# A two-layer HGRN2 and sliding-window-attention trunk: the framework's order of work taken from its time-line picture

## The chip, the cores and the metric

The kernel runs on one core of a Trainium2 chip. A core has four engines that compute: TensorE (PE, matrix products; its loads of stationary operands are shown apart as PEld), VectorE (DVE), ScalarE (ACT) and GpSimd (POOL). SyncE (SP) starts DMA transfers. Each engine works through a list of its own, in order, and instructions of different engines wait for each other by semaphores. The metric is the time of one execution on the device, in microseconds (us), as the median of the runs; beside it, one execution was recorded by the hardware profiler. All quoted rows come from that profile.

## The reference

x has 512 rows of 1024 numbers, fp32. Two layers (DEPTH = 2) each compute

```python
h = rms_norm(x, g_pre)
proj = jnp.einsum('bsd,de->bse', h, w_in)
q_h, f_h, i_h, z_h, q_a, k_a, v_a, z_a = jnp.split(proj, SPLIT_POINTS, axis=-1)
o_h = hgrn2(q_h, f_h, i_h, lb)
o_h = rms_norm(o_h, g_head).reshape(B, S, HG_WIDTH).astype(z_h.dtype) * jax.nn.silu(z_h)
...
o_a = sliding_window_attention(q_a, k_a, v_a, sinks).astype(z_a.dtype) * jax.nn.silu(z_a)
y = jnp.einsum('bse,ed->bsd', jnp.concatenate([o_h, o_a], axis=-1), w_out)
return x + rms_norm(y, g_post)
```

`w_in` has 6400 columns: 1024 each for the recurrence's queries, forget logits, inputs and gate, 1024 for the attention's queries, 128 each for its keys and values, 1024 for its gate. `w_out` maps 2048 to 1024. The recurrence has 8 heads with a 128 x 128 state, S_t = diag(f_t) S_(t-1) + (1 - f_t) i_t^T and o_t = S_t^T q_t. The attention has 16 query heads and 2 key heads of width 64, a causal window of 128, rotary positions and one sink logit per head.

## The kernel before, in words

**Projections.** All weights come as fp32 pieces of 128 x 512 (`raw`, four buffers). Each piece is split in two parts whose sum is the number: ScalarE rounds it to the matmul's type (`whi`, line 189), VectorE forms the rest (`wlo`, line 190). A ring of nine `whi` and nine `wlo` tiles holds the pieces. The activations are split alike (`hhi`, `hlo`, `ops`). Each product is three matmuls of 128 x 128 by 128 x 512 into a PSUM bank `pj` (line 302, three banks): high by high, high by low, low by high. A `Unit` is one output tile of such a projection; `step` writes the next three matmuls, and two units may run interleaved.

**Order in the program.** `ORDER` gives the order of the slabs in a layer: keys and values, attention queries, recurrence inputs, recurrence forget and query slabs, gates, and pieces of the output projection in between. `merge` mixes the writing of other work with the steps of the projections by weights: the attention (`att_stream`) beside the recurrence's inputs and first forget slab, then the recurrence (`prepare`, `hgrn`) beside the following slabs. A step of the attention is: scores on TensorE (lines 560 and 573, into three PSUM banks `sc`), mask and maximum on VectorE (564, 566, 578, 580, 584), exponential on ScalarE (591), the softmax's sums (595, 596), their multiplication on GpSimd (598), transposition on TensorE (604), a split of the result (350, 351), a mask on GpSimd (616), and the value product on TensorE (630, into two PSUM banks `ac`), which lines 632 and 636 bring to SBUF. Per layer there are 16 such steps; the scores of one, the transposition of an earlier and the value product of a still earlier one are written side by side.

Work on weights is planned by `plan_conversions`: a piece's split is due 20 steps ahead of its first use, and pieces at least 3 steps apart. At the seam of the two layers (`seam`) the order of all engines is written out by hand in a string of 100-odd short names.

**Order on the chip.** The program is written for the tile framework. It records the instructions with their dependences, and when the context closes, it settles the order of each engine's list, the buffers of the tiles and the semaphores. To do so, it plays the program through in a picture of the machine: whenever an engine is free there, it gets that instruction, among those whose inputs are ready in the picture, which has the highest priority, and that is the one written earliest. Two things limit this. `pin` keeps an instruction behind everything that is written before it on its engine:

```python
def pin(ins):
    return tc.keep_in_program_order(ins)
```

and `tc.high_priority(n)` makes it count as written n places earlier (mask and maximum of the attention, the evacuation of some projections). Pinned are all of the attention's, the recurrence's and the transposing matmuls, the start of the kernel (`first_kv`) on its engines, and in the seam also the projections' matmuls. Not pinned are the projections' matmuls elsewhere, nearly all weight splits, and most of the work of VectorE, ScalarE and GpSimd. The chip itself follows the lists as they are: an engine whose next instruction has to wait does nothing else meanwhile.

## Time and profile before

| | |
|---|---|
| time, median of 2 runs | 903.64 us (903.6 to 903.68) |
| profiled execution, its time | 904.02 us |
| its span, first to last instruction | 902.3 us |
| busy: PE, PEld, DVE, ACT, POOL | 893.0, 747.7, 650.7, 472.3, 256.5 us |
| granted TensorE clock, mean | 0.998 |
| instructions | 18581 |
| DMA | 102.82 MB, mean 114 GB/s |

The first part of the page gives each engine's busy time, the second the same in 40 slices, and the fourth the chain of work that ended last, followed back from the end. A row of a group of instructions names line, engine, operation, what is written and read, the shape and the count, then busy time, mean ns of one, and the idle time of the engine just before with the instruction that ended it. A row of waits reads: who waited, for whom, us in total, number of times, longest. The time line's rows give start, length, engine, line, operation. PE's ends are modelled, so its records overlap.

### The profile page before, as it was taken

To read this page: it belongs to the slowest core of one execution; us is meant where nothing else is said; L and a number is where in the kernel's file an instruction comes from. 1 tells how busy PE (TensorE), PEld (TensorE's weight loads), DVE (VectorE), ACT (ScalarE), POOL (GpSimd) and SP (SyncE) were. 2 spreads that over 40 slices of the span, in tenths; PEclk is the share of its full clock that TensorE was granted. 3 is DMA by queue.
4 is the path that set the end of the run, shared out by engine and by line. 5 is a ranking of instruction groups with operands and counts; after the bars stand their busy time and mean duration, and the time that the engine had idled before them with its cause. 6 is when DMAs were issued, how large, how long until landed. Compare 5 with 4: busy or idle time off the path is not lost.

```text
span 902.3 us, 18581 instructions
## 1 busy us (share of the span) xinstructions
PE 893.0 (99%) x7206; PEld 747.7 (83%) x7206; DVE 650.7 (72%) x1179; ACT 472.3 (52%) x1067; POOL 256.5 (28%) x233
## 2 busy tenths in 40 slices
PE   9999999999999999999999999999999999999996
PEld 7888888888888888888898888888888888888885
DVE  5888987989666785555777787877767558666556
ACT  6536767754665323534464376686356463145242
POOL 0135445204313123021332344450124121330102
PEclk9999999999999999999999999999999999999999
DMA  9683712322222222434347455222322322223413
GB/s 307 222 225 117 211 46 72 105 94 80 77 82 70 94 82 63 128 119 132 116 153 217 128 164 163 71 80 76 115 72 61 105 71 86 70 73 93 140 36 140
DMA packets 57144, 102.82 MB, mean 114 GB/s; under 512 B 6624, under 2 KB 9184, under 8 KB 57056
## 3 DMA queue, kind: packets, MB, share of 16 engines
q1 hardware_dynamic: 56768, 101.50, 37.2%
q8 instruction: 57, 0.93, 0.4%
q14 instruction: 31, 0.25, 0.1%
q10 hardware_dynamic: 288, 0.14, 0.1%
HBM read 89.03 MB, written 12.58 MB: 113 GB/s over the span
## 4 chain that ended last, share of the span: by engine, by line
PE 95%; DVE 3%; ACT 1%; issue 0%; POOL 0%; POOLq 0%; DVEq 0%; ACTq 0%
PE pj L302 77%; PE ac L630 3%; PE sc L573 2%; PE sc L771 2%; PE ac L840 2%; PE ac L1140 1%; PE sc L604 1%; PE ac L843 1%; PE ac L827 1%; PE sc L902 1%; PE sc L815 1%; PE ac L712 1%; PE sc L560 1%; PE sc L1117 1%; DVE wlo L190 0%; PE sc L775 0%
## 5 line engine op out<-in xcount | busy, mean ns | idle before, releaser
L189 ACT CAST whi<-raw 128x512 fp32r<-128x512 f32 x256 | 155.5, 621 | 126.9 <-PE pj L302 113.4
L190 DVE TENSOR_TENSOR wlo<-raw,whi 128x512 fp32r<-128x512 f32 x253 | 184.1, 746 | 43.4 <-ACT whi L189 42.3
L302 PE MATMUL pj<-hhi,wlo 128*128 128x512 f32 x512 | 202.4, 396 | 0.0
L302 PE MATMUL pj<-hhi,whi 128*128 128x512 f32 x512 | 199.9, 390 | 0.0
L302 PE MATMUL pj<-hlo,whi 128*128 128x512 f32 x512 | 199.4, 389 | 0.0
L302 PE MATMUL pj<-whi,ops 128*128 128x512 f32 (+1 forms) x520 | 172.1, 395 | 0.0
L302 PEld LDWEIGHTS pj<-whi,ops 128*128 128x128 f32 x520 | 97.2, 188 | 19.6 <-DVE y L925 0.3
L302 PEld LDWEIGHTS pj<-hhi,whi 128*128 128x128 f32 x512 | 96.1, 188 | 20.6
L302 PEld LDWEIGHTS pj<-hhi,wlo 128*128 128x128 f32 x512 | 96.2, 188 | 19.3
L302 PEld LDWEIGHTS pj<-hlo,whi 128*128 128x128 f32 x512 | 96.3, 188 | 18.9
L302 PE MATMUL pj<-whi,hlo 128*128 128x512 f32 x256 | 102.9, 404 | 0.0
L302 PE MATMUL pj<-wlo,ops 128*128 128x512 f32 (+1 forms) x260 | 100.7, 387 | 0.0
L302 PE MATMUL pj<-wlo,hhi 128*128 128x512 f32 x256 | 100.1, 391 | 0.3 <-DVE wlo L190 0.3
L302 PE MATMUL pj<-whi,hhi 128*128 128x512 f32 x256 | 100.2, 391 | 0.0
L790 POOL TENSOR_TENSOR k<-k,tot 128x512 f32<-128x512 f32 x40 | 58.0, 1473 | 107.5 <-PE sc L771 51.8
L591 ACT ACTIVATE s<-sc,negm 128x128 f32<-128x128 f32 x128 | 45.6, 370 | 33.4 <-DVE negm L584 25.7
L302 PEld LDWEIGHTS pj<-whi,hhi 128*128 128x128 f32 x256 | 48.0, 188 | 10.3
L302 PEld LDWEIGHTS pj<-wlo,ops 128*128 128x128 f32 x260 | 49.0, 188 | 8.8
L302 PEld LDWEIGHTS pj<-wlo,hhi 128*128 128x128 f32 x256 | 48.3, 189 | 8.7 <-DVE wlo L190 0.8
L302 PEld LDWEIGHTS pj<-whi,hlo 128*128 128x128 f32 x256 | 48.2, 188 | 8.0
L789 DVE TENSOR_TENSOR q<-q,tot 128x512 f32<-128x512 f32 x40 | 37.6, 951 | 20.4 <-PE sc L775 10.9
L598 POOL TENSOR_TENSOR s<-s,sums 128x512 f32<-128x512 f32 x32 | 34.7, 1084 | 52.6 <-DVE sums L596 32.2
(223 smaller groups left out, 1391.4 us busy)
## 6 DMA issues: line engine op xcount, KB each, us to landing
raw<-in_win_dram SPq DMA_DIRECT2D x192, 256.0 KB, 2.7
raw<-in_wout_dram SPq DMA_DIRECT2D x64, 256.0 KB, 2.7
stack<-rot SPq DMA_DIRECT2D x16, 512.0 KB, 3.9
qs<-stack SPq DMA_DIRECT2D x32, 256.0 KB, 4.4
xs<-in_xt_dram SPq DMA_DIRECT2D x8, 256.0 KB, 4.8
raw<-in_wkv_dram SPq DMA_DIRECT2D x8, 256.0 KB, 3.7
a<-in_x_dram SPq DMA_DIRECT2D x8, 256.0 KB, 3.3
x_mid<-a SPq DMA_DIRECT2D x8, 256.0 KB, 2.2
```

What stands on the lines that cost most here:

```text
L189: keep(nc.scalar.copy(hi, v))
L190: keep((nc.gpsimd if i in on_pool and i % 2 else nc.vector).tensor_tensor(lo, v, hi.bitcast(F32), op=ALU.subtract))
L302: ins = nc.tensor.matmul(u.o, lhsT=u.sta(k, u.w)[i], rhs=u.mov(k, u.w)[j], start=(n == 0), stop=(n == len(u.list) - 1))
L560: pin(nc.tensor.matmul(S[:, h * P:(h + 1) * P], lhsT=q[:, h, t_], rhs=kst[v][p][:, 0:P], start=(h == 0 and p == 0), stop=(h == 3 and p == 1)))
L573: pin(nc.tensor.matmul(S[:, h * 256:(h + 1) * 256], lhsT=q[:, 2 * hp_ + h, t_], rhs=kst[v][p][:, (n - 1) * P:(n + 1) * P], start=(h == 0 a ...
L591: nc.scalar.activation(pt[:, h * P:(h + 1) * P], cur[h], AF.Exp, bias=negm[:, h:h + 1], scale=SCALE, accum_out=sums[:, h:h + 1])
L598: nc.gpsimd.tensor_tensor(pv, pv, sums.unsqueeze(2).broadcast_to([P, 4, P]), op=ALU.mult)
L630: pin(nc.tensor.matmul(U, lhsT=vst[v][:, blk, :], rhs=d, start=(i == 0), stop=(i == len(terms) - 1)))
L771: pin(nc.tensor.matmul(L[32 * b:32 * b + 32, c:c + 16], lhsT=k[:, o_ + 32 * b:o_ + 32 * b + 32], rhs=qv[:, blk:blk + qu, 1, :], start=True ...
L789: nc.vector.tensor_tensor(qv[:, :, 1, :], qv[:, :, 1, :], tv[:, :, 0].unsqueeze(2).broadcast_to([P, 2 * nb, hh]), op=ALU.mult)
L790: nc.gpsimd.tensor_tensor(kv_[:, :, 0, :], kv_[:, :, 0, :], tv[:, :, 1].unsqueeze(2).broadcast_to([P, 2 * nb, hh]), op=ALU.mult)
L840: pin(nc.tensor.matmul(O[:, c], lhsT=A[:, c], rhs=vs(j, n), start=(n == 0), stop=False))
```

## The change

The context is opened with another picture of the machine. Nothing of the traced program differs: the same instructions with the same operands, dependences, pins and priorities go in. What comes out, the order of each engine's list, the buffer that each tile gets, and the semaphore waits that follow, is settled by playing the program through in the framework's time-line picture, which follows each instruction through the devices that it holds one after the other (its sequencer, its queue, its engine, its writing back), in place of the simple picture, which is the default.

```diff
-    with tile.TileContext(nc) as tc:
+    with tile.TileContext(nc, schedule_with_timeline_sim=True) as tc:
         hybrid_kernel(tc, *args)
```

## The prediction

> **What bounds the kernel now.** I read the page's first part first, the busy time of each engine, and then the chain that ended last.
>
> ```profile
> span 902.3 us, 18581 instructions
> PE 893.0 (99%) x7206; PEld 747.7 (83%) x7206; DVE 650.7 (72%) x1179; ACT 472.3 (52%) x1067; POOL 256.5 (28%) x233
> ...
> PE 95%; DVE 3%; ACT 1%; issue 0%; POOL 0%; POOLq 0%; DVEq 0%; ACTq 0%
> ```
>
> TensorE (PE) is busy for 893.0 of 902.3 us, and it holds 95% of the chain. The other engines have room on the average: VectorE 28% of the span, ScalarE 48%. So the kernel is one long line of matmuls, and 902.3 - 893.0 = 9.3 us is all the idle time that TensorE has. The next view, the busy time by stretches of the span, says where those 9.3 us lie (rows of the stretches in which TensorE was not full; columns: PE, weight loads, DVE, ACT, POOL, then clock, DMA share and GB/s).
>
> ```profile
> 0.00:22.00 22.00, 20.47 (x120) 17.54 (x121) 11.34 (x18) 14.63 (x23) 0.69 (x6) 1.00 0.93 308
> ...
> 100.00:150.00 50.00, 49.76 (x265) 41.59 (x264) 42.47 (x101) 33.14 (x113) 25.51 (x23) 1.00 0.35 96
> ...
> 450.00:503.00 53.00, 52.76 (x300) 46.16 (x299) 37.91 (x62) 24.91 (x49) 13.28 (x11) 1.00 0.65 193
> 503.00:550.00 47.00, 46.48 (x246) 39.05 (x245) 41.56 (x98) 30.08 (x105) 22.66 (x20) 1.00 0.49 148
> ...
> 890.00:902.30 12.30, 5.54 (x36) 4.89 (x34) 7.54 (x15) 2.47 (x8) 3.52 (x4) 0.83 0.38 129
> ```
>
> Idle: 1.53 us at the head, 0.24 and 0.52 us in the two stretches with attention, 0.24 us at the seam between the layers, and 6.76 us behind the last matmul. These make 9.29 us. Head and end are chains of dependences (the first weights must land; the last tile must be normed and stored), so a new order can reach at most 0.24 + 0.24 + 0.52 = 1.0 us of plain idle time.
>
> A matmul can also wait inside its busy time, because the ends of the records are modelled. A bound for that comes from the eight groups of projection matmuls, which should all last alike:
>
> ```profile
> L302 PE MATMUL pj<-hhi,wlo 128*128 128x512 f32 x512 | 202.4, 396 | 0.0
> L302 PE MATMUL pj<-hhi,whi 128*128 128x512 f32 x512 | 199.9, 390 | 0.0
> L302 PE MATMUL pj<-hlo,whi 128*128 128x512 f32 x512 | 199.4, 389 | 0.0
> L302 PE MATMUL pj<-whi,ops 128*128 128x512 f32 (+1 forms) x520 | 172.1, 395 | 0.0
> ...
> L302 PE MATMUL pj<-whi,hlo 128*128 128x512 f32 x256 | 102.9, 404 | 0.0
> L302 PE MATMUL pj<-wlo,ops 128*128 128x512 f32 (+1 forms) x260 | 100.7, 387 | 0.0
> L302 PE MATMUL pj<-wlo,hhi 128*128 128x512 f32 x256 | 100.1, 391 | 0.3 <-DVE wlo L190 0.3
> L302 PE MATMUL pj<-whi,hhi 128*128 128x512 f32 x256 | 100.2, 391 | 0.0
> ```
>
> Against the lowest mean, 387 ns, the others lie 9, 3, 2, 8, 17, 0, 4 and 4 ns higher; times their counts that is 4.6 + 1.5 + 1.0 + 4.2 + 4.4 + 0 + 1.0 + 1.0 = 17.7 us. I take this as the most that hidden waits hold. The largest surplus, 17 ns, is that of the group that opens each step of the slabs beside the attention.
>
> **Is TensorE really full?** The chain, read in order of time, has a stretch without any other kind of work:
>
> ```profile
> 162.33 36.04 PE pj L302 x159
> ```
>
> 36.04 us / 159 = 227 ns from one projection matmul to the next, undisturbed. With 188 ns of weight load for each (below) the loads fill 188 / 227 = 83%, which is the 83% of the whole span. So 83% of weight-load time is what a gapless stream shows here.
>
> [...]
>
> **The change part by part.** It removes and adds no instruction, tile or DMA. It only replaces the picture in which the framework plays the program through to settle the order of each engine's list: at each moment an engine is given the earliest-written piece that is ready in that picture. So three things can move: the order on each engine, which buffer a tile gets, and thereby who waits for whom.
>
> *TensorE.* Same 7,206 matmuls, 0 us of work gained or lost. In the list that the kernel before was compiled to, only 111 of TensorE's 5,572 instructions stand outside the order in which they are written (all transposes, attention and recurrence matmuls are pinned behind what is written before them, and at the seam the projections too). A new picture finds little to move here; value 0, ends 0 and the waits below.
>
> *VectorE and ScalarE.* Here 439 of 1,180 and 294 of 895 stand out of the written order, so these lists depend on the picture and will change. Where TensorE does not wait for them, that costs nothing: cover is the stream of projection matmuls. Where is the cover thin? The waits of TensorE and of the weight split, and those of one line:
>
> ```profile
> PE sc L573 <- ACT s L591: 0.4, 2, 0.2
> PE pj L302 <- DVE wlo L190: 0.3, 1, 0.3
> ...
> ACT whi L189 <- PE pj L302: 113.4, 68, 7.6
> ...
>   ACT s L591: 4.3, 16
> ```
>
> The third row is good news: 68 times, 113.4 us in all, ScalarE's split waited until TensorE let go of a weight buffer. The splits run up against the end of their ring of buffers, so weights are seldom what TensorE lacks (0.3 us, once). The last row is from the view of the attention's score matmuls (L573): their weight loads and matmuls waited 16 times, 4.3 us in all, for the exponentials (L591) to give back one of three score banks. This is the tight place: 16 steps of attention a layer, 32 in all, each a round of score, mask, maximum, exponential, transpose and value product over four engines, in two stretches of about 100 us. The time line there shows how one piece in front costs:
>
> ```profile
> 96.84 0.53 PEld L573 LDWEIGHTS sc<-kst,qs 128*128 128x128 f32 x4 [0.21 <-ACT s L591]
> ...
> 100.47 1.52 DVE L190 TENSOR_TENSOR wlo<-raw,whi 128x512 fp32r<-128x512 f32 x1
> ...
> 101.38 0.21 ACT L594 ACTIVATE es<-ds 128x4 f32<-128x4 f32 x1
> ...
> 101.92 0.15 DVE L595 TENSOR_TENSOR sums<-sums,es 128x4 f32<-128x4 f32 x1
> ```
>
> The score matmul lost 0.21 us to the exponential; a weight split, 1.52 us long here, stood in front of the sums of the softmax, which could have begun at 101.59 (101.38 + 0.21) and began at 101.92. Mean lengths of such pieces:
>
> ```profile
> L190 DVE TENSOR_TENSOR wlo<-raw,whi 128x512 fp32r<-128x512 f32 x253 | 184.1, 746 | 43.4 <-ACT whi L189 42.3
> ...
> L189 ACT CAST whi<-raw 128x512 fp32r<-128x512 f32 x256 | 155.5, 621 | 126.9 <-PE pj L302 113.4 <-DMA raw<-in_win_dram 8.6 <-ACT ops L904 1.2
> ...
> L302 PEld LDWEIGHTS pj<-hhi,wlo 128*128 128x128 f32 x512 | 96.2, 188 | 19.3
> ```
>
> Price of the new order in the attention, from both sides. Below: all the waits that the order can reach go, -1.0 - 17.7 = -18.7 us. Above: in each of the 32 steps one split of 0.746 us comes to stand in front of a hop of the round and nothing covers it, 32 x 0.746 = +23.9 us. I take a value near the nearest row: as much again as the round costs today, +4.3 us. The reason for a plus: the round's order depends on the picture most, and today's list leaves it only 4.3 us of loss in about 200 us, so there is more to lose than to win.
>
> *GpSimd and SyncE.* SyncE's list is nearly as written (38 of 373 out of order), GpSimd's too (36 of 230). Their cover is the 28% and the ring of raw weights; 0 us, with ends inside those above. *Head, seam and end* are pinned or a single chain: 0 us.
>
> **Sum**, against the profiled execution: span 902.3 + 0 (work) + 4.3 (attention) = 906.6 us; with the 904.02 - 902.3 = 1.7 us around the span 908.3 us. The profiled execution lies 0.4 us above the median of 903.64, so on the median the forecast is 907.9, **908 us**.
>
> **The rivals.**
> 1. *The change does nothing*: both pictures give the same or an equivalent order. Then 903.6 us. For it: TensorE's order is nearly the written one and TensorE sets the time. Against it: 439 instructions of VectorE depend on the picture. Chance 0.15; it is also a result within 2%.
> 2. *Slower: the attention round comes to wait for weight splits.* VectorE is 83% to 88% busy in the attention (42.47 of 50, 41.56 of 47 us), so a split set ahead of a mask or a maximum isn't made up for at once; the score bank comes back later and the in-order TensorE list stands. One uncovered split of 0.746 us in each of 32 steps gives 903.6 + 23.9 = 927.5 us, +2.6%. It decides above 18 us, that is from 24 of the 32 steps on. Against it: the splits run ahead of their use, so the picture sees no hurry for them, and the mask and maximum carry a raised priority. Chance 0.25.
> 3. *Faster: the new picture is nearer to the chip and removes the waits.* All of them gone: 903.6 - 18.7 = 884.9 us, -2.1%. For it: waits are there. Against it: it needs every one of them, and 17.7 us is an upper bound that includes differences of other origin. Chance 0.03; half of it, 894 us, is inside 2%.
> [...]
>
> **How the numbers follow.** 2% of 903.6 is 18.1 us, about what a measurement of this kernel can tell from no change: faster is below 885.6, slower above 921.7. Forecast (0.57, from 896 to 921) and rival 1 (0.15) lie within 2%: 0.72. Slower 0.25, faster 0.03. The likeliest case's own range is 898 to 918 us. The range for 8 in 10 reaches to rival 2's full price and a little past it, 930 us, and down to 898 us, about a third of the way to the removal of all waits.
>
> **What would show each step.** TensorE's busy time within some us of 893 and a gapless stretch at 227 ns: the work is unchanged. The list of VectorE and ScalarE in the attention differs, that of TensorE hardly: the change acts where I say. The waits of L573 for L591: about 9 us instead of 4.3 by the forecast, 25 us or more by rival 2, near 0 by rival 3. The wait of L302 for the weight split stays below 1 us; if it grows to several us, the ring of weight buffers isn't the cover that I take it for. The prediction would be wrong if the new picture moves TensorE's own list, so that projection matmuls run out before the recurrence or the attention is done, or if SyncE's list delays raw weights: then idle time would show in stretches that have none now.

## The result, and the profile after

The kernel with the time-line picture takes 933.91 us (median; 931.66 to 936.17) against 903.64 us: a ratio of 1.0335, 95% interval 1.0228 to 1.0442. It is slower by 30 us, beyond the end of the forecast's range (930 us). The profiled execution took 931.66 us, its span is 929.9 us, so 27.6 us of span are to be explained.

The page of the kernel after: span, busy time, the slices of PE and of its granted clock, the chain's shares, and one group of projection matmuls.

```profile
span 929.9 us, 18580 instructions
PE 901.9 (97%) x7206; PEld 752.6 (81%) x7206; DVE 658.1 (71%) x1179; ACT 481.8 (52%) x1075; POOL 258.5 (28%) x233
...
PE   9999999799999999999999999986999999999997
PEclk9999999799999999999999999997999999999999
...
PE 80%; DVE 9%; ACT 6%; issue 3%; DMA 2%; POOL 0%; POOLq 0%; DVEq 0%; SPq 0%; ACTq 0%
...
L302 PE MATMUL pj<-hhi,wlo 128*128 128x512 f32 x512 | 202.6, 397 | 3.3 <-ACT q L697 2.6
```

The work is the same: 7,206 matmuls, and the group that had 396 ns a matmul has 397. TensorE's share of the chain fell from 95% to 80%. Its idle time grew from 9.3 to 929.9 - 901.9 = 28.0 us (+18.7), its busy time from 893.0 to 901.9 us (+8.9): together the 27.6 us. The two dips in the PE line stand at the 8th slice and at the 27th and 28th, and the clock line dips beside them. The busy time by stretches (PE, PEld, DVE, ACT, POOL, then clock, DMA share, GB/s) of the kernel after:

```profile
0.00:22.00 22.00, 20.46 (x124) 17.40 (x125) 10.71 (x18) 14.07 (x22) 0.68 (x6) 1.00 0.90 304
...
150.00:200.00 50.00, 42.60 (x190) 33.70 (x189) 40.96 (x85) 30.20 (x83) 21.58 (x19) 0.90 0.18 53
...
450.00:503.00 53.00, 52.76 (x299) 46.08 (x298) 43.87 (x72) 28.75 (x64) 16.53 (x15) 1.00 0.51 168
...
600.00:650.00 50.00, 40.00 (x177) 30.43 (x176) 37.36 (x84) 34.61 (x87) 22.96 (x22) 0.86 0.15 43
...
890.00:930.00 40.00, 33.23 (x166) 27.80 (x164) 24.57 (x45) 14.49 (x32) 7.33 (x8) 0.96 0.30 99
```

and the two stretches in question of the kernel before, in which TensorE had no gap:

```profile
150.00:200.00 50.00, 50.00 (x346) 41.33 (x345) 40.62 (x70) 34.85 (x57) 10.35 (x11) 1.00 0.31 95
600.00:650.00 50.00, 50.00 (x343) 41.12 (x341) 38.01 (x63) 29.36 (x53) 9.28 (x9) 1.00 0.32 95
```

Head (1.54 us idle), seam (0.24) and tail (6.77) are as before. The new idle time is 7.40 us in 150 to 200 and 10.00 us in 600 to 650: the end of the attention in each layer, 17.4 of the 18.7 us. No other engine is full there either: VectorE, the busiest of them, is at 82% and 75%. PE's waits of the kernel after (who waited, for whom, us in total, times, longest):

```profile
PE ac L630 <- DVE negm L584: 3.0, 2, 2.7
PE pj L302 <- ACT q L697: 2.6, 1, 2.6
PE sc L573 <- ACT s L591: 2.4, 2, 1.7
PE sc L604 <- DVE a L351: 2.2, 1, 2.2
...
PE sc L604 <- POOL s L598: 2.0, 2, 1.5
```

All of these but the second are hops of the attention's round. The second is the first projection behind the bunch in layer 2, which waits for the recurrence's queries (L697) to be brought out of their PSUM bank. The time line of PE at the end of the first layer's attention shows it:

```profile
167.81 0.73 PE L630 MATMUL ac<-pcur,vst 128*128 128x512 f32 x2 [0.45 <-POOL pcur L616]
168.38 0.40 PE L630 MATMUL ac<-a,vst 128*128 128x512 f32 x1
169.47 0.80 PE L630 MATMUL ac<-a,vst 128*128 128x512 f32 x1 [0.69 <-DVE a L351]
170.06 1.06 PE L630 MATMUL ac<-pprev,vst 128*128 128x512 f32 x2
170.92 1.91 PE L573 MATMUL sc<-kst,qs 128*128 128x256 f32 x8
172.63 1.05 PE L604 MATMUL sc<-ident,s 128*128 128x128 f32 x4
175.41 2.07 PE L573 MATMUL sc<-kst,qs 128*128 128x256 f32 x8 [1.72 <-ACT s L591]
177.28 1.05 PE L630 MATMUL ac<-pcur,vst 128*128 128x512 f32 x2
```

No projection matmul (L302) stands among them. Before, the waits for VectorE, ScalarE or GpSimd had projections to fill them (PE busy for 50.00 of 50 us in both stretches); here TensorE has only attention next in its list and stands still until the round comes back. The last score matmul (L573) of layer 1 starts at 177.1 us instead of 141.5, that of layer 2 at 629.0 instead of 587.8.

The lists as compiled say the same. Counted as the least number of instructions that would have to move to restore the written order, out of it now stand 844 of TensorE's 5,572 instructions (before: 111), 532 of VectorE's 1,180 (439), 363 of ScalarE's 895 (294), 51 of SyncE's 373 (38), 48 of GpSimd's 230 (36). In each layer the last score matmul stood behind the 399th projection matmul; now it stands behind the 504th. There, 46 attention matmuls stand in a row with no projection between them (34 scores and value products in layer 1, 30 in layer 2, the rest transposes), where the longest such row was 16 and 8.

### The profile page after: what moved, and what is told of

The parts are those of the page before. It is cut to its first block, busy times and chain, and to the rows that moved or that the text cites. A ratio compares the mean times of both kernels' runs of the same rounds, so it can differ in the third digit from the quotient of the medians.

```text
span 929.9 us, 18580 instructions
## 1 busy us (share of the span) xinstructions
PE 901.9 (97%) x7206; PEld 752.6 (81%) x7206; DVE 658.1 (71%) x1179; ACT 481.8 (52%) x1075; POOL 258.5 (28%) x233
## 4 chain that ended last, share of the span: by engine, by line
PE 80%; DVE 9%; ACT 6%; issue 3%; DMA 2%; POOL 0%; POOLq 0%; DVEq 0%; SPq 0%; ACTq 0%
PE pj L302 64%; DVE wlo L190 2%; PE sc L771 2%; PE ac L630 2%; PE sc L573 2%; PE ac L840 2%; ACT s L591 1%; PE ac L1140 1%; PE ac L843 1%; PE ac L827 1%; ACT whi L189 1%; PE sc L604 1%; DVE oa L636 1%; PE sc L902 1%; ACT L591 1%
## 5 line engine op out<-in xcount | busy, mean ns | idle before, releaser
L190 DVE TENSOR_TENSOR wlo<-raw,whi 128x512 fp32r<-128x512 f32 x253 | 190.3, 774 | 70.3 <-ACT whi L189 68.7
L302 PE MATMUL pj<-hhi,wlo 128*128 128x512 f32 x512 | 202.6, 397 | 3.3 <-ACT q L697 2.6
L302 PE MATMUL pj<-hlo,whi 128*128 128x512 f32 x512 | 200.7, 392 | 0.0
L302 PE MATMUL pj<-hhi,whi 128*128 128x512 f32 x512 | 200.2, 392 | 0.0
L302 PE MATMUL pj<-whi,ops 128*128 128x512 f32 (+1 forms) x520 | 168.9, 392 | 0.0
L302 PEld LDWEIGHTS pj<-hhi,wlo 128*128 128x128 f32 x512 | 96.7, 189 | 24.0 <-ACT q L697 3.3
L302 PEld LDWEIGHTS pj<-whi,ops 128*128 128x128 f32 x520 | 97.2, 188 | 19.5 <-DVE ops L875 0.4
L302 PEld LDWEIGHTS pj<-hhi,whi 128*128 128x128 f32 x512 | 96.6, 189 | 20.1
L302 PEld LDWEIGHTS pj<-hlo,whi 128*128 128x128 f32 x512 | 96.7, 189 | 18.9
L302 PE MATMUL pj<-wlo,ops 128*128 128x512 f32 (+1 forms) x260 | 101.0, 388 | 0.0
L302 PE MATMUL pj<-wlo,hhi 128*128 128x512 f32 x256 | 100.6, 393 | 0.0
L302 PE MATMUL pj<-whi,hhi 128*128 128x512 f32 x256 | 100.6, 393 | 0.0
L302 PE MATMUL pj<-whi,hlo 128*128 128x512 f32 x256 | 99.9, 392 | 0.0
L598 POOL TENSOR_TENSOR s<-s,sums 128x512 f32<-128x512 f32 x32 | 37.4, 1169 | 93.5 <-DVE sums L596 35.5
L591 ACT ACTIVATE s<-sc,negm 128x128 f32<-128x128 f32 x128 | 45.4, 368 | 29.8 <-DVE negm L584 29.5
L302 PEld LDWEIGHTS pj<-wlo,ops 128*128 128x128 f32 x260 | 48.9, 188 | 9.1
L302 PEld LDWEIGHTS pj<-whi,hhi 128*128 128x128 f32 x256 | 48.1, 188 | 9.6
L302 PEld LDWEIGHTS pj<-wlo,hhi 128*128 128x128 f32 x256 | 48.1, 188 | 9.6
L302 PEld LDWEIGHTS pj<-whi,hlo 128*128 128x128 f32 x256 | 48.0, 188 | 9.5
```

Source lines behind the costliest of these rows:

```text
L190: keep((nc.gpsimd if i in on_pool and i % 2 else nc.vector).tensor_tensor(lo, v, hi.bitcast(F32), op=ALU.subtract))
L302: ins = nc.tensor.matmul(u.o, lhsT=u.sta(k, u.w)[i], rhs=u.mov(k, u.w)[j], start=(n == 0), stop=(n == len(u.list) - 1))
L591: nc.scalar.activation(pt[:, h * P:(h + 1) * P], cur[h], AF.Exp, bias=negm[:, h:h + 1], scale=SCALE, accum_out=sums[:, h:h + 1])
L598: nc.gpsimd.tensor_tensor(pv, pv, sums.unsqueeze(2).broadcast_to([P, 4, P]), op=ALU.mult)
```

## The experiments

Theory A: TensorE's own list is the loss; attention that is listed late ends in a bunch without cover. Theory B: the lists of the other engines are the loss, by making each round longer, as in the forecast. All ratios are to the kernel before, with a 95% interval; it was run again beside each group of kernels (medians 903.44 to 903.94 us), and differences in us are to those runs.

A list is forced, where the text says so, by a dependence of order only (no semaphore) between neighbours of one engine's list; the picture then settles the other engines' lists around it:

```diff
         hybrid_kernel(tc, *args)
+        listed(tc)
...
+        for before, ins in zip(names, names[1:]):
+            tc.add_manual_dep(known[ins], before, mybir.DependencyInfo(mybir.DependencyClass.NoSync, mybir.DependencyReason.DATA),
+                              reason="listed")
```

### Which engine's list: four kernels

**e1** takes the time-line picture with TensorE's list pinned to the written order; **e2** has the same list of TensorE and the simple picture.

```diff
-            if state["pinned"]:
+            if True:
                 pin(ins)
```

> Time-line picture, but every projection matmul (L302) pinned too, so that TensorE's list is the written order and only the other engines' lists come from the new picture. Theory A (TensorE's list is the cause: projections are listed ahead of the attention and run out before it ends): the loss goes, 900 to 910 us, TensorE's idle time in the two attention stretches under 2 us, granted clock back at 0.998. Theory B (the lists of VectorE, ScalarE, GpSimd and SyncE are the cause): stays above 920 us.

> Simple picture with TensorE's list in the written order too: the control for the run before it, with the same TensorE list, instruction for instruction. Theory A: 900 to 910 us. The difference between the two is then what the new picture's lists of the other four engines do by themselves: within 5 us of zero by theory A, about +27 us by theory B.

**x1** takes the simple picture and forces on TensorE the list of the kernel after.

> Simple picture, with TensorE's list of the changed kernel forced on it instruction for instruction; the other lists settle around it in the simple picture. Theory A: as slow as the changed kernel, 925 to 940 us, with TensorE idle near 150-200 and 600-650 us. Theory B: near 904 to 912 us, because the other lists come from the simple picture.

**e4** takes the time-line picture and pins projection matmuls only while the attention is being written.

```diff
+            state["pinned"] = True
             merge((att_stream([(g, n) for g in range(4) for n in range(NT)]), ...), rest(("in", l, FQ)))
+            state["pinned"] = False
```

> Time-line picture, with the projection matmuls pinned only while the attention is written (the first merge of each layer), free after it. Theory A with its place in the attention: 900 to 912 us. If the loss comes from the recurrence or the output projection, it stays above 920 us.

Measured: e1 923.58 us, 1.0217 (1.0198 to 1.0237); e2 913.67, 1.0108 (1.0091 to 1.0125); x1 935.05, 1.0350 (1.0334 to 1.0365); e4 920.10, 1.0183 (1.0168 to 1.0198).

x1 puts a price on it: under the simple picture, TensorE's list of after costs 935.05 - 903.79 = 31.3 us, all that was lost. The other lists were free to settle around it, and did: as compiled, 309 of VectorE's and 214 of ScalarE's instructions stand otherwise than before. So x1 prices TensorE's list together with what it makes the others do. Its two stretches show the same holes:

```profile
150.00:200.00 50.00, 42.01 (x188) 34.34 (x187) 36.59 (x79) 29.09 (x81) 19.64 (x19) 0.90 0.19 53
600.00:650.00 50.00, 39.90 (x167) 30.53 (x166) 36.78 (x79) 38.24 (x92) 24.20 (x22) 0.75 0.17 48
```

By their times e1 and e4 missed what theory A expected (900 to 910 and 900 to 912 us). e1 lies where theory B had it, and e4 just above the 920 us of a loss in the recurrence or the output projection. Their traces say where that time went. In e4 (stretches as above):

```profile
22.00:60.00 38.00, 30.45 (x136) 25.09 (x135) 29.02 (x60) 17.43 (x34) 6.96 (x6) 0.89 0.75 234
150.00:200.00 50.00, 49.20 (x225) 40.41 (x224) 40.31 (x75) 37.58 (x74) 15.40 (x15) 1.00 0.29 85
600.00:650.00 50.00, 49.24 (x226) 40.47 (x225) 38.20 (x69) 36.15 (x74) 15.13 (x15) 1.00 0.30 86
```

The holes at the attention's end are gone, 0.8 us idle in each stretch instead of 7.4 and 10.0, as theory A said (e1: 0.75 us in each, under the 2 us that it named). A new loss stands at the start of the first layer's attention, 7.55 us idle from 22 to 60 us (e1: 6.54, e2: 2.95; in the kernel before, none). The recurrence and the output projection show no loss: from 200 to 450 and from 650 to 890 us PE of e4 has no gap. So theory A holds for the holes, and theory B isn't dead: with TensorE's list held equal, the time-line picture (e1) costs 9.9 us more than the simple one (e2). And e2 against before says that even the 111 instructions that the simple picture moves on TensorE, with what the other lists do around them, are worth 913.67 - 903.79 = 9.9 us. PE's longest wait in e1:

```profile
PE sc L560 <- DMA qs<-stack: 8.2, 2, 6.4
```

and the same row in e2:

```profile
PE sc L560 <- DMA qs<-stack: 2.9, 1, 2.9
```

In e1, the first scores (L560) wait for queries that come by a DMA through DRAM. A reader could take the 8.2 - 2.9 = 5.3 us for a fault of VectorE's list (which rotates the queries) or SyncE's (which sends them). The next kernels tried both.

### The other engines' lists

**y1** takes the time-line picture and forces TensorE's list of before. **h1** and **h2** are e1 with, in turn, VectorE's and SyncE's list of e2 forced.

> Time-line picture, with TensorE's list of the kernel before forced on it instruction for instruction (the mirror of x1). Theory A alone (TensorE's list is the whole cause): 902 to 907 us. Theory A+B (the other engines' lists cost some by themselves, as the 10 us between the two runs with the written order say): 910 to 918 us, with the added wait at the start of the attention, around 45 to 70 us and 495 to 520 us.

> As the time-line run with TensorE in the written order (923.6 us), but VectorE's list is that of the simple picture's run with the same TensorE list (913.7 us), instruction for instruction; ScalarE, GpSimd and SyncE settle around it in the time-line picture. If weight splits that stand ahead of the rotary pieces (L531) on VectorE are what delays the queries at the attention's start: 911 to 917 us. If the lists of SyncE or ScalarE are: above 920 us.

> As the time-line run with TensorE in the written order (923.6 us), but SyncE's list (the order of the DMA issues) is that of the simple picture's run with the same TensorE list. If the order of the query transfers and weight loads on SyncE is the cause of the 10 us between the two: 911 to 917 us. If VectorE's list is: above 920 us.

Measured: y1 915.35 us, 1.0126 (1.0110 to 1.0142); h1 920.31, 1.0181 (1.0163 to 1.0199); h2 920.21, 1.0176 (1.0158 to 1.0194).

y1 gives the other lists their price: 915.35 - 903.94 = 11.4 us, in the range expected, though not at the start of the attention as expected: up to 60 us PE is as busy as before, and 5.6 us of the idle time stand between 60 and 160 us and 2.7 us between 503 and 606 us. This is the loss that the forecast had in mind, and it shows where the forecast looked, in the view of L573:

```profile
  ACT s L591: 10.9, 15
```

10.9 us instead of 4.3, a rise of 6.6 us. Neither h1 nor h2 comes down to the 911 to 917 us of a single cause; both lie just above 920 us, where each was to point at the other's list. Of e1's 9.9 us they took back some 3.3 and 3.7 us (1.0217 to 1.0181 and 1.0176), and h1's interval still touches e1's. Neither list alone carries it; this stays divided.

**y2** and **y3** are y1 with one more list of before forced: VectorE's and ScalarE's.

> Time-line picture with TensorE's and VectorE's lists of the kernel before forced on it; ScalarE, GpSimd and SyncE settle around them in the new picture. The mirror run with TensorE's list alone took 915.35 us, 11.4 us above before. If VectorE's list (weight splits ahead of masks, maxima and rotary pieces) is what is left: 903 to 907 us. If ScalarE's or SyncE's is: 911 us or more.

> The same with TensorE's and ScalarE's lists of the kernel before; VectorE, GpSimd and SyncE settle around them in the new picture. If ScalarE's list (roundings of weights ahead of the exponentials that give back the score banks) is what is left: 903 to 907 us. If VectorE's is: 911 us or more.

Measured: y2 912.88 us, 1.0097 (1.0082 to 1.0112); y3 910.05, 1.0071 (1.0056 to 1.0086). Of the 1.26%, ScalarE's list takes back 0.55 points, some 5 us, with its interval clear of y1's; VectorE's takes back 0.29 points, some 2.6 us, with an interval that still touches. Neither came down to the 903 to 907 us of a single cause. L573's waits in y3:

```profile
  ACT s L591: 7.8, 17
```

In y2 they are 8.0 us in 16 times, nearly the same. In the attention itself the two lists are worth alike: from 60 to 160 and from 503 to 606 us PE is idle for 8.3 us in y1, 4.4 in y2 and 4.6 in y3. What sets y2 back is a wait that y1 and y3 don't have, most of 2.85 us of idle time from 22 to 60 us:

```profile
PE pj L302 <- DVE rot L510: 2.8, 2, 2.1
```

The rest is with the lists that were not forced, or shared.

### Does a buffer limit the projections?

Behind the 504th projection matmul of layer 1, the next one waits for an evacuation of the recurrence's forget slab (`f`, line 426; its weight load waited 0.4 us); in layer 2 it waits for one of the recurrence's queries (`q`, line 697; 2.6 us). The tile of `f` shares four buffers (`fk`) with the keys and values that the attention still holds. By theory A a fifth buffer should let the projections of layer 1 run on. Room for it comes from two of the four raw weight buffers; **g1** is the control without them, **g2** has the fifth buffer, both with the time-line picture.

```diff
-RAW_BUFS = 4
+RAW_BUFS = 2
```

and, in g2 alone:

```diff
-FB = 4
+FB = 5
```

> Time-line picture, two buffers of raw weights instead of four: the control for the run after it, which needs the space. TensorE's list still stops projecting at the 504th projection matmul of each layer, so theory A expects the changed kernel's time, 930 to 945 us, with a little more for the shorter queue of weights.

> As the control, with five instead of four buffers for the tiles that keys, values, forget gates and k share. In layer 1 TensorE's list now stops at the 552nd projection matmul instead of the 504th: 48 matmuls more, 10.9 us at 227 ns, lie beside the attention's end. In layer 2 it still stops at the 504th. Theory A with its second half (projections stop because their results have no buffer to go to while the attention holds them): 5 to 11 us below the control, all of it in layer 1 (150-200 us), the stretch of layer 2 unchanged. If the stop has another cause: within 3 us of the control.

Measured: g1 970.05 us, 1.0733 (1.0717 to 1.0749); g2 965.64, 1.0689 (1.0671 to 1.0707). Both are misses. The control itself cost another 36 us. That late raw weights are the reason is argued, not shown, from ScalarE's waits for them, in g1:

```profile
ACT whi L189 <- DMA raw<-in_win_dram: 121.7, 78, 5.3
```

and the same row of the kernel after:

```profile
ACT whi L189 <- DMA raw<-in_win_dram: 15.5, 14, 3.5
```

The fifth buffer moved the bunch in layer 1 from the 504th projection to the 552nd, so the buffer does set the place where projections stop there. But 42 attention matmuls still stood in a row (54 in g1). In layer 2 the place stayed the 504th, and there too the row became shorter, 42 instead of 58. Only 4.4 us came back, less than the 5 to 11 expected and more than the 3 us of another cause. What makes the bunch isn't this buffer alone.

### Late, or bunched?

In the kernel after, the attention is both late and bunched. Two kernels under the simple picture take these apart, by forced lists of TensorE made from that of before. **s1** stretches the attention (from the 399th to the 444th projection for the last score, from the 465th to the 524th for the last value product) and keeps projections between its pieces (the longest row without any stays 16, as before; the 12 of the expectation doesn't hold for the list as compiled). **b1** leaves the early attention in its place and puts what stood behind the 372nd to the 465th projection together behind the 465th: 62 attention matmuls in a row, 42 of them scores and value products. That is a longer row than the 46 of the kernel after.

> Simple picture, with TensorE's list of before changed in one way: from the 172nd projection matmul of a layer on, the attention's matmuls stand 1.2 times as far along the projections, evenly (the last score behind the 444th projection matmul instead of the 399th, the last value product behind the 524th instead of the 465th); nowhere do more than 12 of them stand together. If lateness of the attention is what costs: 45 to 59 matmuls of 227 ns a layer, 10 to 13 us, so 915 to 930 us in all. If only rounds without projections between them cost: 900 to 908 us.

> Simple picture, with TensorE's list of before changed in one way: the attention's matmuls that stand behind the 372nd to the 465th projection matmul of a layer all stand behind the 465th, 42 of them together, as 34 and 30 do behind the 504th in the changed kernel. Nothing before them is moved. If rounds without projections between them are the loss: 10 to 16 us a layer, 922 to 936 us, with TensorE idle and its granted clock lowered just there, and the rest of the kernel as before. If the loss needs the new lists of the other engines: below 912 us.

Measured: s1 910.02 us, 1.0071 (1.0055 to 1.0088); b1 929.40, 1.0285 (1.0269 to 1.0300). The two stretches in s1:

```profile
150.00:200.00 50.00, 46.80 (x214) 38.14 (x213) 42.45 (x82) 37.76 (x74) 14.09 (x14) 1.00 0.27 80
600.00:650.00 50.00, 48.20 (x219) 39.19 (x218) 41.46 (x76) 37.47 (x76) 15.08 (x14) 1.00 0.29 85
```

and in b1:

```profile
150.00:200.00 50.00, 41.55 (x182) 33.13 (x182) 35.44 (x71) 30.82 (x63) 15.93 (x16) 0.93 0.15 46
600.00:650.00 50.00, 40.92 (x180) 32.22 (x179) 29.84 (x61) 29.11 (x62) 15.01 (x15) 0.93 0.14 43
```

with these waits of PE in b1:

```profile
PE sc L573 <- ACT s L591: 6.3, 4, 2.9
PE ac L630 <- POOL pcur L616: 6.1, 2, 3.1
PE sc L604 <- POOL s L598: 4.1, 2, 2.1
```

Lateness with cover costs 6.6 us (5.0 us idle in the two stretches, clock 1.00). It is a smaller lateness than that of the kernel after: the last score comes 45 projections later, there 105. The bunch without any lateness ahead of it costs 26.0 us, leaves 8.45 + 9.08 = 17.5 us of holes like the 17.4 of the kernel after, in the same two stretches, on hops of the same round, and with a lower clock. In b1 the other lists are nearly those of before (as compiled, 43 of VectorE's and 44 of ScalarE's instructions stand otherwise, none of SyncE's), so here the other lists can hardly be the reason. So the bunch is the cause: x1 puts the whole list in, b1 only a bunch, and in e1 and e4, where TensorE's list has no such row, the holes at the attention's end are gone. No run takes the bunch alone out of the list of after, and since b1's row is longer, its 26.0 us are not that bunch's exact price.

## Why the prediction was wrong

- **TensorE, "a new picture finds little to move here; value 0": this step failed.** It read the 111 instructions out of written order as a sign that TensorE's list hardly depends on the picture. But that count belongs to the simple picture alone; the projection matmuls are free to move between the pinned pieces, and with the other picture 844 instructions stand out of order. Nor was 111 a small thing: writing the list out without them costs 9.9 us (e2). The new list, with the other engines' lists settling around it, costs 31.3 us (x1), and a bunch alone 26.0 us (b1). The prediction named this as what would make it wrong ("projection matmuls run out before the recurrence or the attention is done"), and gave it no price. What it lacked is a term for that: it measured 7.40 + 10.00 us of standing still, one hole a layer, and on top the lower clock, 0.50 for 10.24 and 13.65 us.
- **Attention round, +4.3 us: right mechanism, mis-sized, and not the one that decided.** With TensorE's list held it measured +11.4 us (y1), and the waits of L573 for L591 went to 10.9 us where "about 9" was forecast. So the round did get longer, by ScalarE's list and by VectorE's about alike (y3, y2). This term and TensorE's don't add: 31.3 + 11.4 us is more than the 30 us lost. In the kernel after, those waits are 6.2 us in 7 times.
- **Rival 2, 927.5 us** had the right side and nearly the size, by another mechanism: one uncovered split in each of 32 steps. The trace shows a few long waits at two places, not 32 short ones.
- **SyncE and GpSimd, 0:** for SyncE not borne out in e1, where its list of the simple picture took back some 3.7 us (h2). Under the list of after nothing shows it.
- **Head, seam and end, 0: right.** Idle there is the same to 0.01 us.
- **Weights not lacking: right.** No wait of L302 for a weight split is among the waits of the kernel after.
- **Two readings of the prediction are off.** VectorE's share in the attention is 85% to 88%, not 83% to 88% (42.47 of 50 us is 85%). And 17.7 us is no upper bound of the hidden waits, since it takes the fastest group of matmuls to have none; that end of the range was never reached.
- **A gapless stretch at 227 ns: right.** In the chain of the kernel after, one goes at 21.99 / 97 = 227 ns a matmul, as before:

```profile
650.85 21.99 PE pj L302 x97
```

- **Busy time within some us of 893:** 901.9, with 7,206 matmuls as before; of the 8.9 us more, about 8.6 are the lower clock's, by the estimate of the last section.

**What stays open.** Why the time-line picture lists TensorE's attention late. That it comes late shows on VectorE, whose maximum (L578) hardly waited for the scores of L573 in the kernel before:

```profile
  DVE sc L578: 0.6, 1
```

and does in the kernel after:

```profile
  DVE sc L578: 13.4, 8
```

Whether the picture's durations or its queues do that wasn't tried. Open too are how e1's 9.9 us divide between VectorE, ScalarE and SyncE, and what makes the bunch in layer 2.

## What to carry to other kernels

Where one in-order engine sets the time, its own list is the first thing to compare, and the number of instructions out of written order says nothing of their worth. Look for the longest row of dependent work without independent work between: late but interleaved cost 6.6 us here, in time but bunched 26. No version tried beat the kernel before; the lowest were s1 and y3 at 910.0 us.

## What the hardware showed

The holes cost more than their length, because the granted clock is lower in and behind them. In the kernel after it was 0.50 from 168.7 to 179.0 us (10.24 us) and from 632.9 to 646.6 us (13.65 us), though no wait of PE was longer than 2.7 us. b1 has single stretches at 0.50 of 3.41 us (158.13 to 161.55 and 171.79 to 175.20 us); 10.24 and 13.65 us are three and four times that. The time of the kernel after, cut in pieces of this length at these edges (PE's busy time, clock, DMA share, GB/s):

```profile
161.87:165.29 3.42, 1.98 (x8) 1.00 0.28 81
165.29:168.70 3.41, 1.51 (x7) 1.00 0.51 154
168.70:172.10 3.40, 2.71 (x10) 0.50 0.00 0
172.10:175.50 3.40, 1.68 (x9) 0.50 0.00 0
175.50:178.95 3.45, 3.45 (x12) 0.50 0.02 5
178.95:182.40 3.45, 3.45 (x17) 1.00 0.00 0
...
626.10:629.50 3.40, 2.10 (x12) 1.00 0.00 0
629.50:632.90 3.40, 0.74 (x2) 1.00 0.00 0
632.90:636.30 3.40, 1.97 (x6) 0.50 0.01 2
```

Here a piece in which PE was busy for 58% or 62% was followed by clock 1.00, one with 44% or 22% by 0.50. After a piece at 0.50 with 80% busy (in layer 2 with 95%) the clock stayed there, after one with 100% it rose to 1.00; in other runs it rose once each after 88% (g1) and 78% (g2). The same reading of x1 and b1 gives drops after 40%, 19%, 58% and after 16%, 11%, 28%, and a return after 98% to 100%. In the eight traces that were read so (after, x1, b1, g1, g2, e1, s1, y1), the drops inside the run followed pieces of up to 58%, and the clock stayed at 1.00 after some from 46% on (g2): between 46% and 58% busy both were seen.

PE's busy time within the two stretches at 0.50:

```profile
168.72:178.96 10.24, 7.83 (x28) 6.51 (x28) 7.23 (x23) 4.95 (x21) 3.26 (x4) 0.50 0.01 2
632.93:646.58 13.65, 9.40 (x24) 6.15 (x25) 10.80 (x19) 8.20 (x22) 8.72 (x9) 0.50 0.00 1
```

Projection matmuls follow each other there every 0.43 us (643.12 to 646.10 us, seven steps) instead of 0.227. At clock 1.00 the 7.83 + 9.40 = 17.2 us would thus take about half, an estimate from the clock and these steps, and the other half is 8.6 of the 8.9 us of added busy time. s1, where the clock fell only behind the last matmul (mean 0.998, as in the kernel before), was busy for 893.3 us, nearly as the kernel before (893.0).

The bunch of the kernel after, with waits of up to 2.7 us, is thus paid for in the waits (7.40 + 10.00 us of idle time) and once more in slow matmuls (about 8.6 us, by the estimate above).
